# Part to part in a four-layer trunk: squares summed block by block, the boundary products by segments with the norm between them

## The chip, the cores and the metric

The kernel runs on one core of one Trainium2 chip. A core has a matrix engine (TensorE, PE in the profile), a vector engine (VectorE, DVE), a scalar engine (ScalarE, ACT), a general engine (GpSimd, POOL) and an engine that only issues transfers here (SyncE, SP). Each engine works through its own queue in order and waits on semaphores for the others. The metric is the device time of one execution in microseconds (us), lower is better.

## The reference, cut to what matters

512 tokens of 1024 features (256 of context and 256 latent ones) go through four layers, whose mixers are HGRN2, RWKV-7, MLA and HGRN2. Each layer is a mixer and a convolutional feed-forward part, each behind a norm with a shift, scale and gate of its own, which are computed from a conditioning vector:

```python
mod_l = jnp.split((silu_c @ w_mod[layer] + b_mod[layer])[:, None, :], 6, axis=-1)
h_l = modulate(rmsnorm(x_l, norm1[layer]), mod_l[0], mod_l[1])
y_c, y_l = hgrn2_mixer(h_c, h_l, ...)       # or rwkv7_mixer, or mla_mixer
x_l = x_l + mod_l[2] * y_l
x_l = x_l + mod_l[5] * conv_ffn(modulate(rmsnorm(x_l, norm2[layer]), mod_l[3], mod_l[4]), ...)
```

The context stream does the same with its own modulation; the last layer is needed for the latent tokens alone, and a last norm ends it. `conv_ffn` is a product to twice 2816 features, a convolution over three tokens, a gate and a product back to 1024. So there are eight norms, each of which needs the whole result of the part before it: the mean of squares runs over all 1024 features of a token.

## The kernel before, in words

The residual stream stays on the chip as eight tiles `xT` of 128 features x 512 tokens. Columns 0 to 255 are the context (segment 0), columns 256 to 511 the latent tokens (segment 1). Weights are loaded in single precision and split into a high part (`whi`, a cast on ScalarE, line 431) and a rest (`wlo`, a subtraction on VectorE, line 432); activations are split in the same way (`hh` and `hl`, `uh` and `ul`, `oh` and `ol`). Each product is three matmuls (`mm3`, lines 456 to 458). `dense2` (460) computes two blocks of 128 features for all 512 tokens, eight of 128 deep or eleven; a raw weight tile is `wraw`, in a ring of four.

A norm is `norm_mod` (527), which calls `rstd` (500). ScalarE squares the eight tiles (508); GpSimd adds up tiles 1 to 3, VectorE 5 and 6 (512); 12 matmuls with a column of ones per segment of 256 tokens (24 in all) give the sums (517); five small operations make the reciprocal root (`rsqrt`, 489 to 494); four matmuls spread it over the partitions (524). Then for each tile and segment VectorE scales (549), ScalarE makes `hh` (551) and VectorE `hl` (552). All this stands as a whole between the last product of one part and the first of the next; the residual is `xT[n] += gate * product` (566), on VectorE, as each block's product ends.

A scheduler with a model of the engines orders the instructions of all engines from the program and the rings of buffers; the RWKV scan is ordered by hand. What a ring of buffers allows thus sets how far loads and their users may stand apart.

The first feed-forward part (FFN 0) does two things beside its own work, in steps that `ffn` takes between its products. `presplit` (435) loads and splits RWKV's weights by way of GpSimd's queue (`praw`, `phi`, `plo`) and writes them to device memory. `mod_in_pool` (406) computes the modulation of layer 1: `mod` (383) loads 96 tiles `mraw` of 128x512 on SyncE's queue (396), eight per step, and multiplies each by the 32 columns of `sc` (397). Its ring has eight buffers. The modulation of layer 0 is computed in the same way in the first HGRN part.

## Time and profile before

| | us |
|---|---|
| median of 3 runs | 3153.69 |
| lowest, highest | 3151.88, 3156.07 |
| the profiled execution | 3154.18 |
| span of its trace | 3152.4 |
| TensorE busy | 2875.8 (91%) |
| VectorE busy | 1767.0 (56%) |
| ScalarE busy | 1391.1 (44%) |
| GpSimd busy | 552.2 (18%) |

The parts in the trace: HGRN 0 to 428, FFN 0 to 833, RWKV to about 1633, FFN 1 to 2009, MLA to 2273, FFN 2 to 2649, the last HGRN to 2935, FFN 3 to 3137, the last norm to the end. The rows below come from four views: the page (sums over the execution), a table of stretches (each engine's busy time in a stretch, with the granted TensorE clock as a share of full speed), a timeline of one engine (runs of equal instructions, and in brackets how long the engine stood idle before and for whom), and a list of the instructions of one line. Matmuls overlap in their ends, so the distance of two starts is what one costs.

### The profile page before, as it was taken

Reading aid. Unit: us, or ns where it says so; the run is one execution under the profiler, and the core shown is the slowest. Engines: PE = TensorE matmul, PEld = TensorE weight load, DVE = VectorE, ACT = ScalarE, POOL = GpSimd, SP = SyncE. Lnnn points to the kernel's source line nnn. Section 1 sums busy time; section 2 is a strip of 40 time slices with the busy share of each in tenths; the row PEclk is TensorE's granted clock in tenths of the full one; section 3 lists DMA queues with packets and bytes.
Section 4 is the critical chain, followed back from the end, with each engine's and each line's share of the span. In section 5 each row is a group of like instructions: output and inputs, shape, how many; then the busy total and the mean of one; then the engine's idle time right before and its main releaser. Section 6 shows DMA issues by size and latency. Waiting matters only on the chain. (4 is left out here: it accounts for less than half of the span.)

```text
span 3152.4 us, 52606 instructions
## 1 busy us (share of the span) xinstructions
PE 2875.8 (91%) x20861; PEld 2292.2 (73%) x20861; DVE 1767.0 (56%) x3113; ACT 1391.1 (44%) x2642; POOL 552.2 (18%) x727
## 2 busy tenths in 40 slices
PE   7999999999787787788879999899899999999898
PEld 4588877778575556666658888776578887888898
DVE  4278765445573346866564444466554344488765
ACT  3266643334442145665543223345433233577544
POOL 1023322222442133444310000000000000123000
PEclk9999989999888888988779999899999998999999
DMA  8622168886756865666553332210123332332554
GB/s 282 197 68 68 52 220 269 282 283 221 223 178 200 235 194 156 172 173 182 166 169 94 100 94 91 76 41 30 54 80 101 94 94 80 87 94 77 155 185 127
DMA packets 475336, 452.70 MB, mean 144 GB/s; under 512 B 98492, under 2 KB 415826, under 8 KB 474962
## 3 DMA queue, kind: packets, MB, share of 16 engines
q1 hardware_dynamic: 458352, 398.27, 41.3%
q0 software_dynamic: 15360, 50.34, 4.8%
q8 instruction: 164, 2.69, 0.4%
q10 hardware_dynamic: 1378, 0.73, 0.1%
q14 instruction: 82, 0.67, 0.1%
HBM read 392.64 MB, written 56.10 MB: 142 GB/s over the span
## 5 line engine op out<-in xcount | busy, mean ns | idle before, releaser
L457 PE MATMUL mm<-hl,whi 128*128 128x512 f32 (+1 forms) x2024 | 744.9, 368 | 10.9 <-DVE hl L552 10.9
L456 PE MATMUL mm<-hh,whi 128*128 128x512 f32 (+1 forms) x2024 | 744.8, 373 | 10.3 <-ACT hh L551 6.9
L458 PE MATMUL mm<-hh,wlo 128*128 128x512 f32 (+1 forms) x2024 | 742.4, 368 | 0.0
L432 DVE TENSOR_TENSOR wlo<-wraw,whi 128x1024 fp32r<-128x1024 f32 (+1 forms) x392 | 464.7, 1188 | 428.9 <-ACT whi L431 415.6
L431 ACT CAST whi<-wraw 128x1024 fp32r<-128x1024 f32 (+1 forms) x392 | 395.9, 1013 | 554.0 <-PE mm L457 489.6
L456 PEld LDWEIGHTS mm<-hh,whi 128*128 128x128 f32 x2024 | 386.2, 192 | 91.1 <-issue 10.8
L457 PEld LDWEIGHTS mm<-hl,whi 128*128 128x128 f32 x2024 | 386.0, 191 | 79.2 <-DVE hl L552 14.4
L458 PEld LDWEIGHTS mm<-hh,wlo 128*128 128x128 f32 x2024 | 385.6, 191 | 66.1 <-issue 6.1
L456 PE MATMUL mm<-uh,whi 128*128 128x512 f32 (+1 forms) x704 | 255.2, 363 | 0.0
L457 PE MATMUL mm<-ul,whi 128*128 128x512 f32 (+1 forms) x704 | 255.1, 363 | 0.0
L458 PE MATMUL mm<-uh,wlo 128*128 128x512 f32 (+1 forms) x704 | 254.2, 363 | 0.0
L512 POOL TENSOR_TENSOR t<-t,t 128x512 f32<-128x512 f32 (+1 forms) x27 | 35.2, 1305 | 868.1 <-ACT t L508 866.8
L456 PEld LDWEIGHTS mm<-uh,whi 128*128 128x128 f32 x704 | 132.8, 189 | 24.1 <-issue 2.5
L457 PEld LDWEIGHTS mm<-ul,whi 128*128 128x128 f32 x704 | 132.9, 189 | 20.3
L458 PEld LDWEIGHTS mm<-uh,wlo 128*128 128x128 f32 x704 | 132.5, 189 | 20.6
L449 DVE TENSOR_TENSOR plo<-praw,phi 128x512 fp32r<-128x512 f32 x64 | 45.3, 709 | 171.4 <-ACT phi L448 171.3
L448 ACT CAST phi<-praw 128x512 fp32r<-128x512 f32 x64 | 39.8, 622 | 216.3 <-DMA praw<-in_rw_w_rkv_dram 119.7
L2128 DVE SCALAR_TENSOR_TENSOR t<-mm,prm,t 128x510 f32<-128x510 f32 (+1 forms) x88 | 60.0, 682 | 105.4 <-ACT t L2126 105.4
L566 DVE SCALAR_TENSOR_TENSOR xT<-mm,mod,xT 128x256 f32<-128x256 f32 x176 | 74.4, 478 | 67.2 <-PE mm L458 67.2
L2126 ACT ACTIVATE t<-mm,prm 128x512 f32<-128x512 f32 (+1 forms) x88 | 63.3, 719 | 108.2 <-PE mm L458 108.2
L725 POOL TENSOR_TENSOR t<-t 128x512 f32<-128x512 f32 x32 | 46.4, 1450 | 362.6 <-DVE t L715 319.3
L1889 PE MATMUL md<-mraw,sc 128*32 128x256 f32 x768 | 71.5, 449 | 29.6 <-DMA mraw<-in_w_mod_dram 29.3
(426 smaller groups left out, 5199.7 us busy)
## 6 DMA issues: line engine op xcount, KB each, us to landing
wraw<-in_ffn_w_in_dram SPq DMA_DIRECT2D x176, 512.0 KB
mraw<-in_w_mod_dram SPq DMA_DIRECT2D x192, 256.0 KB
mraw<-in_w_mod_dram SPq DMA_DIRECT2D x96, 512.0 KB
wraw<-in_hg_w_in_dram SPq DMA_DIRECT2D x80, 512.0 KB
wraw<-in_ffn_w_out_dram SPq DMA_DIRECT2D x80, 512.0 KB
ow<-preo SPq DMA_DIRECT2D x64, 256.0 KB
praw<-in_rw_w_rkv_dram POOLq DMA_DIRECT2D x48, 256.0 KB, 4.4
vw<-prev SPq DMA_DIRECT2D x32, 256.0 KB
```

The costliest lines, as they stand in the source:

```text
L431: nc.scalar.copy(h, r)
L432: nc.vector.tensor_tensor(out=w, in0=r, in1=h.bitcast(F32), op=ALU.subtract)
L448: nc.scalar.copy(hi, raw)
L449: nc.vector.tensor_tensor(out=lo, in0=raw, in1=hi.bitcast(F32), op=ALU.subtract)
L456: nc.tensor.matmul(ps, lhsT=wh, rhs=xh, start=start, stop=False)
L457: nc.tensor.matmul(ps, lhsT=wh, rhs=xl, start=False, stop=False)
L458: nc.tensor.matmul(ps, lhsT=wl, rhs=xh, start=False, stop=stop)
L566: nc.vector.scalar_tensor_tensor(out=self.xT[n][:, sl], in0=ps[:, sl], scalar=m[:, which * 8 + n, s:s + 1], in1=self.xT[n][:, sl], op0=ALU ...
L725: nc.gpsimd.tensor_tensor(out=c3(de), in0=b3[:, :, end:end + 1].to_broadcast([P, 8, 64]), in1=b3, op=ALU.subtract)
L1889: nc.tensor.matmul(g["ps"][32 * c:32 * c + 32, halves[f]], lhsT=self.sc[:, k, :], rhs=g["raw", u][:, c], start=k == 0 and f == 0, stop=k = ...
L2126: nc.scalar.activation(c[:, sl], pa[b][:, sl], AF.Identity, bias=self.prm[:, cb + j + b:cb + j + b + 1], scale=w[1])
L2128: nc.vector.scalar_tensor_tensor(out=c3[:, :, 1:], in0=p3[:, :, :255], scalar=w[0], in1=c3[:, :, 1:], op0=ALU.mult, op1=ALU.add)
```

## The change

Four things change. First, as each block's product ends, `settle` adds it to the stream, and squares it at once; the squares of blocks 1 to 5 are added to those of block 0 (`acc`), blocks 6 and 7 keep their own tile. A norm then needs 6 sum matmuls per segment. Second, the last pair of blocks of a part goes by segments (`dense2s`, `last_pairs`; in HGRN `last_few`, all eight blocks of the last two heads), and so does the first product of the next part (`arrive`, and a piece of `hgrn`), so each of these products has 256 columns instead of 512. Third, the norm is a generator, `norm_tail`, one per segment: segment 0's stands among the products of segment 1 that end a part, segment 1's among the products of segment 0 that begin the next. Ahead of RWKV, which needs no split operands, `norm_whole` does the same work by segments. The first norm of all and the one behind RWKV stay as they were. Fourth, the tiles between two parts live in a pool of their own (`nq`), and rings elsewhere are smaller: `wraw` three instead of four in HGRN and MLA, the modulation's `mraw` in FFN 0 four instead of eight, `u` 32 instead of 34, two in HGRN by one; MLA's `p` and `q` share the ring `h`. The diff, without the pieces that only pass names on:

```diff
-HG_T2 = 13
+HG_T2 = 12
...
+    def settle(self, l, which, n, src, segs, last):
+        nc = self.nc
+        m, _ = self.mods[l]
+        sl = slice(SEGS[segs[0]][0], SEGS[segs[-1]][1])
+        x = self.xT[n]
+        for s in segs:
+            q = slice(*SEGS[s])
+            nc.vector.scalar_tensor_tensor(out=x[:, q], in0=src(s), scalar=m[:, which * 8 + n, s:s + 1], in1=x[:, q], op0=ALU.mult, op1=ALU.add)
+        if n == 0 and "acc" not in self.sq:
+            self.sq["acc"] = self.nq.tile([P, NT], F32, tag="acc", name="acc", bufs=1)
+        if n == 0:
+            nc.scalar.activation(self.sq["acc"][:, sl], x[:, sl], AF.Square)
+            return
+        if last:
+            if n not in self.sq:
+                self.sq[n] = self.nq.tile([P, NT], F32, tag="sq", name="sq", bufs=2)
+            nc.scalar.activation(self.sq[n][:, sl], x[:, sl], AF.Square)
+            return
+        if len(segs) == 1:
+            t = self.nq.tile([P, 256], F32, tag="xn", name="xn", bufs=2)
+        else:
+            t = self.nq.tile([P, NT], F32, tag="sq", name="sq", bufs=2)
+        nc.scalar.activation(t, x[:, sl], AF.Square)
+        a = self.sq["acc"]
+        nc.vector.tensor_tensor(out=a[:, sl], in0=a[:, sl], in1=t, op=ALU.add)
...
+    def norm_stat(self, segs, psum):
+        nc = self.nc
+        toks = [j for s in segs for j in (2 * s, 2 * s + 1)]
+        st = psum()
+        for i, (k, sq) in enumerate(self.sq.items()):
+            for j in toks:
+                nc.tensor.matmul(st[:, j:j + 1], lhsT=sq[:, j * P:(j + 1) * P], rhs=self.ones[:, 0:1], start=(i == 0 and j == toks[0]),
+                                 stop=(i == len(self.sq) - 1 and j == toks[-1]))
+        return self.rsqrt(st[:, toks[0]:toks[-1] + 1], [P, len(toks)], 1.0 / D, EPS)
...
+    def norm_spread(self, rr, segs, psum):
+        bc = psum()
+        j0 = 2 * segs[0]
+        for j in range(j0, 2 * segs[-1] + 2):
+            self.nc.tensor.transpose(bc[:, j * P:(j + 1) * P], rr[:, j - j0:j - j0 + 1].to_broadcast([P, P]), self.ident)
+        return bc
...
+    def norm_tail(self, l, w, h, s, psum):
+        nc = self.nc
+        m, g1 = self.mods[l]
+        rr = self.norm_stat([s], psum[0])
+        yield
+        bc = self.norm_spread(rr, [s], psum[-1])
+        sl = slice(*SEGS[s])
+        for k in range(KT):
+            hi, lo = h[k]
+            xn = self.nq.tile([P, 256], F32, tag="xn", name="xn", bufs=2)
+            sh = m[:, 24 * w + k, s:s + 1]
+            nc.vector.scalar_tensor_tensor(out=xn, in0=self.xT[k][:, sl], scalar=g1[:, 8 * w + k, s:s + 1], in1=bc[:, sl], op0=ALU.mult, op1=ALU.mult)
+            nc.scalar.activation(hi[:, sl], xn, AF.Identity, bias=sh)
+            nc.vector.scalar_tensor_tensor(out=lo[:, sl], in0=xn, scalar=sh, in1=hi[:, sl].bitcast(F32), op0=ALU.add, op1=ALU.subtract)
...
+    def leave(self, l, which, segs, nxt, blocks, psum):
+        nl, nw = nxt
+        self.table()
+        h = self.norm_tiles() if nw is not None else None
+        first = iter(())
+        for s in segs:
+            for done in blocks(s):
+                for n, src in done:
+                    self.settle(l, which, n, lambda _: src, [s], n >= KT - 2)
+                next(first, None)
+            for _ in first:
+                pass
+            if s != segs[-1]:
+                first = self.norm_tail(nl, nw, h, s, psum) if nw is not None else iter([self.rr.append(self.norm_stat([s], psum[0]))])
+        if nw is None:
+            self.rr.append(self.norm_stat([segs[-1]], psum[0]))
+        self.next = h
+        self.tail = (lambda psum: self.norm_tail(nl, nw, h, segs[-1], psum)) if nw is not None else None
...
+    def dense2s(self, wap, c0, k0, xs, segs, step, ps=None):
+        v = wap.rearrange("(k p) n -> p k n", p=P)
+        nk = len(xs)
+        g = []
+        for ks in range(0, nk, 4):
+            ke = min(ks + 4, nk)
+            g.append((ks, ke, *self.weights(v[:, k0 + ks:k0 + ke, c0:c0 + 256], ke - ks, 256)))
+        for s in segs:
+            sl = slice(*SEGS[s])
+            p = [self.psmm(), self.psmm()] if ps is None else ps
+            for ks, ke, wh, wl in g:
+                for k in range(ks, ke):
+                    for b in range(2):
+                        self.mm3(p[b][:, sl], wh[:, k - ks, b * P:(b + 1) * P], wl[:, k - ks, b * P:(b + 1) * P],
+                                 xs[k][0][:, sl], xs[k][1][:, sl], k == 0, k == nk - 1)
+                if ke < nk:
+                    yield None
+            yield p
...
+    def arrive(self, wap, c0, segs, psum):
+        tail = self.tail(psum)
+        ps = [self.psmm(), self.psmm()]
+        if len(segs) == 1:
+            for _ in tail:
+                pass
+        for _ in self.dense2s(wap, c0, 0, self.next, segs, None, ps):
+            next(tail, None)
+        for _ in tail:
+            pass
+        return ps
...
-            self.open_w(st)
+            self.open_w(st, 3)
...
                 os_.append(self.hg_read(j, o, g, sl, hp))
-            for h0, h1 in ((0, HG_A), (HG_A, 8)):
-                self.out_proj(l, a["hg_w_o"][j], h0, os_[h0:h1], sl, segs)
+            self.out_proj(l, a["hg_w_o"][j], 0, os_[:HG_A], sl, segs)
+            self.last_few(l, 2, a["hg_w_o"][j], HG_A, os_[HG_A:], segs, (l, 1), [lambda: self.psax("rd", HG_RD), lambda: self.psax("at", HG_AT)],
+                          lambda u: self.psmm() if u < 3 else self.psax("S", HG_S))
...
+    def last_pairs(self, l, which, wap, k0, xs, sl, segs, nxt, psum, step=None):
+        self.sq = {}
+        self.rr = []
+        for nb in range(0, KT - 2, 2):
+            if step:
+                step()
+            ps = self.dense2(wap, nb * P, k0, xs, sl)
+            for b in range(2):
+                self.settle(l, which, nb + b, lambda s, b=b: ps[b][:, slice(*SEGS[s])], segs, False)
+        steps = self.dense2s(wap, (KT - 2) * P, k0, xs, segs, None)
+        def blocks(s):
+            for p in steps:
+                if p is None:
+                    yield ()
+                    continue
+                yield [(KT - 2 + b, p[b][:, slice(*SEGS[s])]) for b in range(2)]
+                return
+        self.leave(l, which, segs, nxt, blocks, psum)
...
+    def last_few(self, l, which, wap, k0, xs, segs, nxt, psum, banks):
+        self.sq = {}
+        self.rr = []
+        v = wap.rearrange("(k p) n -> p k n", p=P)
+        nk = len(xs)
+        g = [self.weights(v[:, k0:k0 + nk, c0:c0 + NT], nk, NT) for c0 in (0, NT)]
+        def blocks(s):
+            sl = slice(*SEGS[s])
+            for u in range(4):
+                ps = banks(u)
+                wh, wl = g[u // 2]
+                for b in range(2):
+                    c = slice((2 * (u % 2) + b) * P, (2 * (u % 2) + b + 1) * P)
+                    for k in range(nk):
+                        self.mm3(ps[:, 256 * b:256 * b + 256], wh[:, k, c], wl[:, k, c], xs[k][0][:, sl], xs[k][1][:, sl], k == 0, k == nk - 1)
+                yield [(2 * u + b, ps[:, 256 * b:256 * b + 256]) for b in range(2)]
+        self.leave(l, which, segs, nxt, blocks, psum)
...
-        t = self.t2("rd", 4)
+        t = self.t2("rd", 3)
...
+    def norm_whole(self, l, tiles):
+        nc = self.nc
+        m, g1 = self.mods[l]
+        for s in range(2):
+            sl = slice(*SEGS[s])
+            bc = self.norm_spread(self.rr[s], [s], self.psax)
+            for k in range(KT):
+                xn = self.t2()
+                nc.vector.tensor_tensor(out=xn[:, sl], in0=self.xT[k][:, sl], in1=bc[:, sl], op=ALU.mult)
+                nc.scalar.activation(tiles[k][:, sl], xn[:, sl], AF.Identity, scale=g1[:, k, s:s + 1], bias=m[:, k, s:s + 1])
+        return tiles
...
+                    ps = self.arrive(W, 0, segs, sc)
+                    h = self.next
                 bc = self.rstd(ps, 256, 1.0 / 256, EPS, [0, 1, 2, 3], ("sc", ML_SC))
                 xs = []
                 for b in range(2):
...
-                    p = self.t2("p", ML_P)
+                    p = self.nq.tile([P, NT], F32R, tag="h", name="p", bufs=16).bitcast(F32)
...
-            nxt = iter(()) if mod is None else self.mod_in_pool(mod, st, 8)
+            nxt = iter(()) if mod is None else self.mod_in_pool(mod, st, 4 if pre else 8)
...
                     next(nxt, None)
                     steps(4)
-                    pa = self.dense2(a["ffn_w_in"][l], j * P, 0, h, sl)
+                    if j or self.tail is None:
+                        pa = self.dense2(a["ffn_w_in"][l], j * P, 0, h, sl)
+                    else:
+                        pa = self.arrive(a["ffn_w_in"][l], 0, segs, ax)
                     ss = []
                     for b in range(2):
...
-                        hi = ap.tile([P, NT], F32R, tag="u", name="uh", bufs=34)
-                        lo = ap.tile([P, NT], F32R, tag="u", name="ul", bufs=34)
+                        hi = ap.tile([P, NT], F32R, tag="u", name="uh", bufs=FF_U)
+                        lo = ap.tile([P, NT], F32R, tag="u", name="ul", bufs=FF_U)
...
                         us.append((hi, lo))
-                for nb in range(0, KT, 2):
+                def step():
                     next(nxt, None)
                     steps(3)
+                if j0:
+                    self.last_pairs(l, 5, a["ffn_w_out"][l], j0, us, sl, segs, nxt_norm, ax, step)
+                    for g in (nxt, spl):
+                        for _ in g:
+                            pass
+                    continue
+                for nb in range(0, KT, 2):
+                    step()
                     ps = self.dense2(a["ffn_w_out"][l], nb * P, j0, us, sl)
```

On TensorE in FFN 0, before, the modulation's products (`ax<-mraw,sc`) stand eight together between the products of the part:

```order
1879 L456 MATMUL mm<-hh,whi 128x512
1880 L457 MATMUL mm<-hl,whi 128x512
1881 L458 MATMUL mm<-hh,wlo 128x512
1882 L397 MATMUL ax<-mraw,sc 32x512 x8
1883 L456 MATMUL mm<-hh,whi 128x512
1884 L457 MATMUL mm<-hl,whi 128x512
1885 L458 MATMUL mm<-hh,wlo 128x512
1886 L456 MATMUL mm<-hh,whi 128x512
```

There are 11 such rows of eight, and two of four around the norm. After the change the same engine has there, a few products apart:

```order
1980 L398 MATMUL ax<-mraw,sc 32x512 x4
1981 L457 MATMUL mm<-hh,whi 128x512
1982 L458 MATMUL mm<-hl,whi 128x512
```

```order
2004 L459 MATMUL mm<-hh,wlo 128x512
2005 L398 MATMUL ax<-mraw,sc 32x512
2006 L457 MATMUL mm<-hh,whi 128x512
2007 L458 MATMUL mm<-hl,whi 128x512
2008 L459 MATMUL mm<-hh,wlo 128x512
2009 L457 MATMUL mm<-hh,whi 128x512
2010 L458 MATMUL mm<-hl,whi 128x512
2011 L398 MATMUL ax<-mraw,sc 32x512
2012 L459 MATMUL mm<-hh,wlo 128x512
2013 L457 MATMUL mm<-hh,whi 128x512
2014 L458 MATMUL mm<-hl,whi 128x512
2015 L398 MATMUL ax<-mraw,sc 32x512
```

Of the 96 products, 12 rows now have four, one three, and 45 one.

On VectorE, at the norm from FFN 1 to MLA, before (the four operations `rs` are the reciprocal root, `t` and `hl` make the operands of the next product, `wlo` is a weight split):

```order
1540 L494 SCALAR_TENSOR_TENSOR rs_18792<-rs_18793,rs_18792 128x4
1541 L549 SCALAR_TENSOR_TENSOR t_18805<-xT_81,g_8615,sc 128x256 x2
1542 L549 SCALAR_TENSOR_TENSOR t_18814<-xT_82,g_8615,sc 128x256 x2
1543 L549 SCALAR_TENSOR_TENSOR t_18823<-xT_83,g_8615,sc 128x256 x2
1544 L549 SCALAR_TENSOR_TENSOR t_18832<-xT_84,g_8615,sc 128x256 x2
1545 L552 SCALAR_TENSOR_TENSOR hl<-t_18805,mod,hh 128x256 x2
```

```order
1555 L552 SCALAR_TENSOR_TENSOR hl<-t_18859,mod,hh 128x256 x2
1556 L552 SCALAR_TENSOR_TENSOR hl<-t_18868,mod,hh 128x256 x2
1557 L432 TENSOR_TENSOR wlo<-wraw,whi 128x1024
```

After the change, from the middle of segment 0's operands to the first of segment 1 (`xn` is what `t` was):

```order
1592 L433 TENSOR_TENSOR wlo<-wraw,whi 128x1024
1593 L623 SCALAR_TENSOR_TENSOR hl<-xn,mod,hh 128x256
1594 L433 TENSOR_TENSOR wlo<-wraw,whi 128x1024
1595 L623 SCALAR_TENSOR_TENSOR hl<-xn,mod,hh 128x256
1596 L621 SCALAR_TENSOR_TENSOR xn<-xT_87,g_8831,ax 128x256
1597 L621 SCALAR_TENSOR_TENSOR xn<-xT_88,g_8831,ax 128x256
1598 L623 SCALAR_TENSOR_TENSOR hl<-xn,mod,hh 128x256 x2
1599 L490 TENSOR_SCALAR rs_19173<-sc 128x2
1600 L493 TENSOR_TENSOR rs_19175<-rs_19174 128x2
1601 L494 SCALAR_TENSOR_TENSOR rs_19175<-rs_19175,rs_19173 128x2
1602 L495 SCALAR_TENSOR_TENSOR rs_19174<-rs_19175,rs_19174 128x2
1603 L621 SCALAR_TENSOR_TENSOR xn<-xT_81,g_8831,sc 128x256
```

Weight splits that stood outside the norm stand between the operands of segment 0, and segment 1's root behind them.

On TensorE, at the end of the first HGRN part, the sums of segment 0 (`ones`) after the change, where `oh` and `ol` are the operands of the last two heads' products:

```order
1737 L457 MATMUL S<-oh,whi 128x256
1738 L458 MATMUL S<-ol,whi 128x256
1739 L459 MATMUL S<-oh,wlo 128x256
1740 L598 MATMUL rd<-ones,acc 128x1 x2
1741 L598 MATMUL rd<-ones,sq 128x1 x4
1742 L606 MATMUL at<-ident,rs_3979 128x128 x2
1743 L457 MATMUL mm<-hh,whi 128x256
```

Before, the products have 512 columns, and the whole norm's sums stood at the same place:

```order
1690 L457 MATMUL mm<-ol,whi 128x512
1691 L458 MATMUL mm<-oh,wlo 128x512
1692 L517 MATMUL ax<-ones,t_3961 128x1 x4
1693 L517 MATMUL ax<-ones,t_3972 128x1 x4
1694 L517 MATMUL ax<-ones,t_3980 128x1 x4
1695 L524 MATMUL ax<-ident,rs_3995 128x128 x4
1696 L397 MATMUL ax<-mraw,sc 32x512 x4
1697 L456 MATMUL mm<-hh,whi 128x512 x4
```

The sums now are six for one segment, and the first product of the next part follows its transposes.

## Rows read from the trace of the kernel before

**Rows 1.** Profile page: busy times, the weight split, one kind of load.
```profile
PE 2875.8 (91%) x20861; PEld 2292.2 (73%) x20861; DVE 1767.0 (56%) x3113; ACT 1391.1 (44%) x2642; POOL 552.2 (18%) x727
...
L432 DVE TENSOR_TENSOR wlo<-wraw,whi 128x1024 fp32r<-128x1024 f32 (+1 forms) x392 | 464.7, 1188 | 428.9 <-ACT whi L431 415.6
...
praw<-in_rw_w_rkv_dram POOLq DMA_DIRECT2D x48, 256.0 KB, 4.4
```
**Rows 2.** Stretches: PE, PEld, DVE, ACT, POOL busy (instructions), clock, DMA share, GB/s.
```profile
450.00:720.00 270.00, 269.21 (x1263) 206.70 (x1262) 130.12 (x175) 97.73 (x133) 57.70 (x107) 1.00 0.81 268
720.00:833.00 113.00, 113.00 (x500) 93.43 (x498) 55.20 (x77) 42.35 (x59) 29.11 (x54) 1.00 0.66 215
2955.00:3136.00 181.00, 181.00 (x1510) 181.00 (x1510) 117.65 (x166) 94.19 (x137) 2.21 (x3) 1.00 0.56 172
```
**Rows 3.** The same view, stretches around the norms.
```profile
428.00:450.00 22.00, 14.72 (x58) 9.66 (x58) 18.80 (x42) 12.96 (x27) 4.96 (x8) 0.64 0.90 309
833.00:858.00 25.00, 6.59 (x30) 5.91 (x29) 17.77 (x28) 16.04 (x32) 16.29 (x23) 0.58 0.99 266
858.00:890.00 32.00, 21.89 (x69) 15.78 (x70) 31.94 (x41) 14.27 (x24) 17.28 (x19) 0.74 0.42 127
2008.00:2034.00 26.00, 15.19 (x55) 12.13 (x54) 18.41 (x38) 13.42 (x28) 4.67 (x3) 0.61 0.18 50
2273.00:2296.00 23.00, 14.13 (x56) 10.95 (x55) 18.89 (x44) 11.11 (x23) 0.00 (x0) 0.63 0.22 69
2649.00:2670.00 21.00, 13.99 (x47) 11.09 (x46) 17.93 (x39) 11.69 (x25) 3.36 (x3) 0.59 0.23 76
2934.00:2951.00 17.00, 10.44 (x60) 9.32 (x60) 12.83 (x28) 8.42 (x19) 2.21 (x3) 0.70 0.41 124
```
**Rows 4.** Timeline of PE, FFN 1 to MLA (start, us, line, count, idle before).
```profile
2008.54 0.39 PE L458 MATMUL mm<-uh,wlo 128*128 128x512 f32 x1
2014.55 1.87 PE L517 MATMUL sc<-ones,t 128*128 128x1 f32 x8 [5.63 <-POOL t L512]
...
2023.07 1.11 PE L524 MATMUL sc<-ident,rs 128*128 128x128 f32 x4 [1.32 <-DVE rs L494]
2025.78 2.07 PE L456 MATMUL mm<-hh,whi 128*128 128x512 f32 x4 [1.59 <-ACT hh L551]
...
2029.39 0.63 PE L457 MATMUL mm<-hl,whi 128*128 128x512 f32 x1
2029.82 0.63 PE L458 MATMUL mm<-hh,wlo 128*128 128x512 f32 x1
```
**Rows 5.** Timeline of DVE, the same stretch.
```profile
2008.29 1.66 DVE L566 SCALAR_TENSOR_TENSOR xT<-mm,mod,xT 128x256 f32<-128x256 f32 x4 [11.34 <-PE mm L458]
2011.61 5.11 DVE L432 TENSOR_TENSOR wlo<-wraw,whi 128x1024 fp32r<-128x1024 f32 x3 [1.66 <-ACT whi L431]
...
2024.30 3.22 DVE L549 SCALAR_TENSOR_TENSOR t<-xT,g,sc 128x256 f32<-128x256 f32 x8 [1.29 <-PE sc L524]
```
**Rows 6.** Timeline of PE: modulation products, two, one and eight (two records each).
```profile
106.83 1.05 PE L397 MATMUL at<-mraw,sc 128*32 128x512 f32 x4
...
108.61 0.40 PE L458 MATMUL mm<-hh,wlo 128*128 128x512 f32 x1
108.94 1.04 PE L397 MATMUL at<-mraw,sc 128*32 128x512 f32 x2
109.91 0.50 PE L456 MATMUL mm<-hh,whi 128*128 128x512 f32 x1
...
491.31 0.39 PE L458 MATMUL mm<-hh,wlo 128*128 128x512 f32 x1
491.63 1.92 PE L397 MATMUL ax<-mraw,sc 128*32 128x512 f32 x16
493.48 0.50 PE L456 MATMUL mm<-hh,whi 128*128 128x512 f32 x1
```
**Rows 7.** Stretches as in rows 2: the heads of the last HGRN.
```profile
2670.00:2934.00 264.00, 249.88 (x1879) 219.21 (x1878) 189.30 (x350) 165.70 (x358) 62.31 (x81) 0.98 0.30 88
```

More of the change, by code (lines that the diff above doesn't have):

```diff
@@ new lines, in norm_tiles @@
+    def norm_tiles(self):
+        return [tuple(self.nq.tile([P, NT], F32R, tag="h", name="h" + n, bufs=16) for n in "hl") for _ in range(KT)]
+    def leave(self, l, which, segs, nxt, blocks, psum):
[16 more added lines that the diff above has]
+        self.tail = (lambda psum: self.norm_tail(nl, nw, h, segs[-1], psum)) if nw is not None else None
@@ L837, in hg_scan @@
         return o
+    def norm_whole(self, l, tiles):
+        nc = self.nc
+        m, g1 = self.mods[l]
+        for s in range(2):
+            sl = slice(*SEGS[s])
[5 more added lines that the diff above has]
+        return tiles
     def rwkv(self, l, segs):
@@ L898, in rw_project @@
         pp = st.enter_context(tc.tile_pool(name="pa", bufs=1, reuse_waits="tile"))
-        h = self.norm_mod(l, 0, [0, 1], None, None, tiles=[pp.tile([P, NT], F32, name=f"ph{i}") for i in range(KT)])
+        h = self.norm_whole(l, [pp.tile([P, NT], F32, name=f"ph{i}") for i in range(KT)])
         dx = []
@@ L2110, in ffn @@
             self.tp = st.enter_context(self.tc.tile_pool(name="ft", bufs=8, reuse_waits="tile"))
-            h = self.norm_mod(l, 1, segs, ap2(ap, 16), "h")
+            ax = [self.psax]
+            if self.tail is None:
+                h = self.norm_mod(l, 1, segs, ap2(self.nq, 16), "h")
+            else:
+                h = self.next
             def steps(n):
@@ L2154, in final @@
             op = st.enter_context(self.tc.tile_pool(name="eo", bufs=1, reuse_waits="tile"))
[L2155 to L2156 removed]
+            bc = self.norm_spread(self.rr[0], [1], self.psax)
             ot = [op.tile([P, D], F32, name=f"ot{j}") for j in range(2)]
@@ L2203, in trunk @@
         t.consts()
+        keep = ExitStack()
+        t.open_n(keep)
         for l in range(DEPTH):
             segs = [0, 1] if l < DEPTH - 1 else [1]
+            before = l + 1 < DEPTH and (l + 1) % 3 == 1
             if l % 3 == 0:
@@ L2208, in trunk @@
             elif l % 3 == 1:
+                keep.close()
                 t.rwkv(l, segs)
+                t.open_n(keep)
             else:
                 t.mla(l, segs)
-            t.ffn(l, segs, l + 1 if l + 1 < DEPTH and l + 1 not in t.mods else None, (l + 1) % 3 == 1 and l + 1 < DEPTH)
+            t.ffn(l, segs, l + 1 if l + 1 < DEPTH and l + 1 not in t.mods else None, before, (l + 1, None if before or l + 1 == DEPTH else 0))
+        keep.close()
         with ExitStack() as st:
```

54 lines of the change are left out of this document (39 added, 15 removed).

## The prediction

> **What bounds the kernel now.** I read the page's list of busy times first: TensorE is busy for 91% of the span, VectorE for 56% [rows 1]. An average says nothing about a place, so the second view is the table by stretches. Inside a sub-layer TensorE has no idle time at all: 269.21 of 270 us in the first channel mixer up to 720 us, 113.00 of 113 after it, 181.00 of 181 in the last one [rows 2]. There an instruction added to TensorE costs its whole time. The stretches around the norms are the opposite: from the last product of a sub-layer to the first products of the next, TensorE does little and its granted clock falls to between 0.58 and 0.74 [rows 3]. The timeline of one of them shows why [rows 4]: last product at 2008.54, the sum-of-squares matmuls at 2014.55 after 5.63 us idle for GpSimd's additions, the transposes at 2023.07, the first product at 2025.78, and then products 0.43 apart, where they are 0.226 apart before (113 us for 500 [rows 2]).
>
> How much each norm costs is the stretch minus the products in it. From [rows 3], with 28 (the 24 sums and 4 transposes of a norm) taken off each count: FFN 1 to MLA has 55 - 28 = 27 products, 27 x 0.226 = 6.1, so 26.0 - 6.1 = 19.9 us are lost. In the same way MLA to FFN 2 loses 23.0 - 28 x 0.226 = 16.7 and FFN 2 to the last HGRN 21.0 - 19 x 0.226 = 16.7. HGRN 0 to FFN 0 has 58 - 28 - 16 = 14 products and one set of eight modulation products (1.9 us, below): 22.0 - 3.2 - 1.9 = 16.9. FFN 0 to RWKV loses nearly all of 25.0 and then 32.0 - 69 x 0.226 = 16.4 more. Last HGRN to FFN 3, one segment: 60 - 12 - 2 = 46 products of 0.12 (181 us for 1510 [rows 2]), so 17.0 - 5.5 = 11.5.
>
> **The norms, gain.** In the order of the change, at FFN 1 to MLA, segment 0's sums and transposes stand among the products of segment 1, the transposes four products before the last one; its VectorE work then runs while TensorE ends the old product and starts the new one. What is late next is VectorE. Between the transposes of segment 0 and segment 1's first operand its queue holds 16 operations of 128x256, two residuals and three weight splits, as the VectorE rows of the change show in part. Durations: 8 of the 128x256 kind take 3.22 us and 4 residuals 1.66 [rows 5], so 0.40 and 0.41 each; a weight split takes 1.19 [rows 1]. 16 x 0.40 + 2 x 0.41 + 3 x 1.19 = 10.8. To it come the chain of reciprocal root, 1.3 (TensorE's idle time before the transposes [rows 4]), the sums and transposes of one segment, about 0.6 (estimate, a half of the 1.11 of four transposes and little more), and VectorE's and ScalarE's first operand, 0.40 each: 2.7. Less the 0.5 by which the transposes stand ahead, segment 1's first product comes 13.0 us after the last old one. In between TensorE has the 48 products of segment 0, 48 x 0.12 = 5.8. Lost: 7.2, and I add 2.0 for products at the lower clock (about ten at 0.43 for 0.226 [rows 4]): 9.2. Before, the three weight splits lay in the wait for GpSimd [rows 5]; now they stand in the chain that TensorE waits for. Gains: FFN 1 to MLA 19.9 - 9.2 = 10.7; MLA to FFN 2 and FFN 2 to HGRN, with like queues, 7.5 each.
>
> HGRN 0 to FFN 0 gets less: there segment 0's sums stand behind the very last product, so its chain (2.0) and its 16 operations are not covered by segment 1's products: 2.0 + 6.4 + 3.6 + 1.2 (two splits of half the size) + 2.7 = 15.9, less 5.8, plus 2.0 = 12.1: gain 4.8. FFN 0 to RWKV: VectorE is the bound from 858 to 890 (31.94 of 32 [rows 3]); from 833 to 890 it is busy 49.7 of 57, so 7.3 can be gained there, and about 2 more by the additions that move ahead: 9. Last HGRN to FFN 3 has no second segment to cover its norm: 0. The last norm saves its square additions, about 1. Sum: 10.7 + 15 + 4.8 + 9 + 0 + 1 = 40.5. For a bound from below: the 2 us of clock may be 4 in four places and the queues of VectorE may wait for ScalarE's casts, so 28; from above, below under the rivals, 63.
>
> **The modulation products, loss.** The change halves the ring of their weight tiles in the first channel mixer. 96 such products of 32 columns are there. Before, 88 of them stand outside the norm in 11 sets of eight side by side (16 records a set [rows 6], two for each). In the order of the change the second four of each eight wait for a buffer, and are spread: 58 groups instead of 13, namely 12 of four, one of three, and 45 alone, one of four being in the slack of the norm. The price of each stands in the trace. Eight together: from the product before at 491.31 to the product after at 493.48 are 2.17 us, less the 0.23 of a pair without them: 1.94. One alone, in layer 0 between the same kind of products: 108.61 to 109.91 is 1.30, less 0.23: 1.07; two side by side take no longer, 1.05 for 1.04 [rows 6]. From two on each adds some 0.15 (1.94 for eight), so a group of four is near 1.35, and one of three near 1.2. Before: 11 x 1.94 = 21.3. After: 45 x 1.07 + 11 x 1.35 + 1.2 = 64.2. Difference 42.9, in a stretch where nothing is idle [rows 2]. The groups near the ends of the part may have a wait to stand in: 40. Bounds: 30 if a part stands in waits that are there anyway, 45 where groups lie close together.
>
> **Their loads.** Twelve sets of four loads now wait for TensorE to free the ring, and the weight loads behind them on SyncE's queue wait too. A load of the same 256 KB takes 4.4 us on GpSimd's queue [rows 1]. The DMA engines are 0.81 busy there [rows 2]. If each set is waited for in full, 12 x 4.4 = 53; if none, 0. The first single stands 25 rows, some 5.7 us, behind its four, so I am near the lower end: 4.
>
> **Split products.** The order has 516 products of 512 columns fewer and 1032 of 256 more. A pair of 0.12 is 0.24 for 0.226: 516 x 0.014 = 7, of which some stand in the stretches counted above: 5. Bounds 0 and 13. The Trainium skill, "TensorEngine Tiling (Array Packing)", Instruction Overhead, gives each matmul an overhead of about 60 cycles; at the upper clock of 2.4 GHz 516 more would by that be 13 us (an estimate from that page). The rows at 0.12 and 0.226 show half as much, and the sum goes by them.
>
> **Smaller rings in HGRN and MLA** (weights 4 to 3, two others by one). Over the heads of the last HGRN TensorE is idle for 264.0 - 249.9 = 14.1 us [rows 7], so its tiles are mostly there early. A buffer less can delay, and another order can help: -3 to 8, taken as 2.
>
> **Sum.** Against the profiled execution of 3154.18 us (span 3152.4 and 1.8 around it; the median of the runs is 3153.69, 0.5 less): 3154.2 + 40 + 4 + 5 + 2 - 40 = 3165. I forecast 3165 us, slower by 0.35%. About 0.2%, 6.3 us, is what a measurement of this kernel can tell from no change. Its own range, by the bounds of the terms taken together, is 3152 to 3182.
>
> **Rivals.**
> Faster (other side): the clock. If the products of segment 0 are enough that the granted clock stays at full, and the weight splits slip into VectorE's gaps, each of the three wide boundaries loses about 5 us rather than 9.2, HGRN 0 to FFN 0 also 5, and FFN 0 to RWKV gains 12: 14.9 + 11.7 + 11.7 + 11.9 + 12 + 1 = 63. Then 3154.2 + 51 - 63 = 3142. It decides for faster once the gains pass 57. For it: the last HGRN to FFN 3, with the shortest idle times, shows 0.70, FFN 0 to RWKV 0.58 [rows 3]. Against: it fell there too, after a wait of about 6 us, and 13.0 us with 5.8 of products leave a longer one. The Trainium skill, "TensorE: Matmul & The Clock Gate", What's actually happening, says that the array is throttled by default and that activity releases it: by that rule filling the gap keeps the clock, which is this rival. The trace agrees that the clock falls in every norm, and no row shows it with the gap half filled.
>
> Loads waited for: TensorE's queue is in order, and a modulation product whose load is late holds all behind it. At three quarters of the 53: 3165 - 4 + 40 = 3201, say 3200. For it: DMA is 0.81 busy. Against: the scheduler has put the singles some microseconds behind the fours.
>
> No change that counts: the singles cost less than the row shows, since the products around them, in a denser stretch, are ready to go (0.8 a group: 46 - 21 = 25), and the gains are as summed: 3154.2 + 25 + 11 - 38 = 3152. Against: the row of 1.30 was taken among just such products.
>
> **Chances.** Forecast 0.52, faster by the clock 0.20, no change 0.15, loads 0.13. The forecast's own spread (3152 to 3182) puts a fifth of it, 0.09, within 6.3 us, and 0.03 of the no-change case lies below: faster 0.23, same 0.21, slower 0.56. The range is 3143 to 3195: it reaches to the clock's 3142 but not past it, and short of the full wait for loads.
>
> **What would show it.** In the profile after: isolated modulation products between products 1.30 us apart, and the first channel mixer longer by some 40; the stretch from the last product of FFN 1 to full rate in MLA shorter by about 10, with TensorE waiting for VectorE's segment 1 and a granted clock below 1; no idle time for GpSimd's additions. Wrong would be: singles that cost 0.3 to 0.5, a clock of 1 across the norms, or TensorE waiting for the modulation loads in microseconds.

## The result, and the profile after

The changed kernel takes 3187.5 us (median of 4 runs, 3180.8 to 3192.4), the kernel before 3152.8: 1.0108 times as long, 95% interval 1.0085 to 1.0131. The profiled execution took 3192.37, with a span of 3190.7, so it is the slowest of the four.

Where the time went shows in the distance from the last product of a part to the last product of the next (starts of these products, from the timelines of TensorE; each part holds the norm at its start):

```
us              HGRN 0  FFN 0   RWKV  FFN 1    MLA  FFN 2  HGRN 3  FFN 3
before           428.0  404.8  797.3  378.4  264.6  376.1   285.9  201.9
after            421.6  452.4  796.7  382.2  269.8  371.9   281.1  200.7
difference        -6.4  +47.6   -0.6   +3.8   +5.2   -4.2    -4.8   -1.2
```

FFN 0 alone lost more than the whole kernel. The stretches of the changed kernel that answer to [rows 2, 3], shifted with the parts (span, then busy time and instructions of PE, PEld, DVE, ACT, POOL, then clock, DMA share, GB/s):

```profile
421.00:443.00 22.00, 11.92 (x74) 10.71 (x73) 15.56 (x34) 9.95 (x20) 3.34 (x7) 0.74 0.81 273
450.00:720.00 270.00, 270.00 (x1121) 180.02 (x1120) 119.43 (x160) 92.64 (x126) 57.83 (x108) 1.00 0.78 257
720.00:874.00 154.00, 154.00 (x722) 121.76 (x721) 74.83 (x112) 57.14 (x82) 32.72 (x64) 1.00 0.62 203
874.00:899.00 25.00, 6.68 (x26) 3.84 (x24) 22.63 (x40) 14.18 (x28) 13.55 (x17) 0.59 0.98 251
899.00:931.00 32.00, 26.88 (x102) 20.67 (x103) 31.94 (x33) 15.22 (x24) 18.41 (x11) 0.89 0.35 116
2053.00:2079.00 26.00, 21.70 (x139) 19.60 (x138) 19.42 (x43) 13.64 (x28) 0.00 (x0) 0.93 0.29 84
2323.00:2346.00 23.00, 18.65 (x110) 16.86 (x109) 18.19 (x41) 12.34 (x24) 0.00 (x0) 0.85 0.30 94
2695.00:2716.00 21.00, 15.23 (x102) 14.52 (x103) 16.46 (x37) 11.11 (x23) 2.48 (x8) 0.84 0.24 76
2976.00:2993.00 17.00, 10.21 (x70) 9.69 (x70) 14.44 (x31) 9.77 (x18) 0.00 (x0) 0.80 0.54 173
```

Two things are to be seen. In the 270 us from 450, TensorE is busy throughout as before, but weight loads fell from 1262 to 1120 [rows 2]: fewer products in the same time, with no engine to wait for. And around the wide norms TensorE is busier: 21.70 of 26 us where it was 15.19 [rows 3], with a granted clock of 0.93 for 0.61.

In between stand the lone modulation products, on TensorE in FFN 0:

```profile
551.64 0.39 PE L459 MATMUL mm<-hh,wlo 128*128 128x512 f32 x1
551.96 1.05 PE L398 MATMUL ax<-mraw,sc 128*32 128x512 f32 x2
552.94 0.50 PE L457 MATMUL mm<-hh,whi 128*128 128x512 f32 x1
553.27 0.39 PE L458 MATMUL mm<-hl,whi 128*128 128x512 f32 x1
...
554.29 1.04 PE L398 MATMUL ax<-mraw,sc 128*32 128x512 f32 x2
555.27 0.50 PE L459 MATMUL mm<-hh,wlo 128*128 128x512 f32 x1
```

From 551.64 to 552.94 is 1.30 us, as in layer 0 before [rows 6]. Groups of four cost the same 1.31, not the 1.58 (1.35 and 0.23) of my estimate; why is in the last section. No product here waits for its load. At FFN 1 to MLA, which answers to [rows 4]:

```profile
2052.33 0.38 PE L606 MATMUL ax<-ident,rs 128*128 128x128 f32 x2
...
2052.90 0.28 PE L459 MATMUL mm<-uh,wlo 128*128 128x256 f32 x1
2056.26 0.58 PE L457 MATMUL mm<-hh,whi 128*128 128x256 f32 x1 [3.08 <-DVE xn L621]
...
2062.73 0.50 PE L598 MATMUL sc<-ones,acc 128*128 128x1 f32 x4
2063.09 1.03 PE L598 MATMUL sc<-ones,sq 128*128 128x1 f32 x8
...
2065.53 0.40 PE L606 MATMUL sc<-ident,rs 128*128 128x128 f32 x2
2067.05 0.97 PE L457 MATMUL mm<-hh,whi 128*128 128x256 f32 x4 [1.11 <-ACT hh L622]
```

Segment 0's transposes stand before the last old product (2052.90), its first new product comes 3.4 us after it, segment 1's 14.1 us after it; the prediction had 13.0. GpSimd's wait is gone. On VectorE the operands of segment 0 and the weight splits stand close behind each other up to segment 1's reciprocal root:

```profile
2060.49 1.22 DVE L433 TENSOR_TENSOR wlo<-wraw,whi 128x1024 fp32r<-128x1024 f32 x1
2061.62 0.48 DVE L623 SCALAR_TENSOR_TENSOR hl<-xn,mod,hh 128x256 fp32r<-128x256 f32 x1
2062.02 0.87 DVE L621 SCALAR_TENSOR_TENSOR xn<-xT,g,ax 128x256 f32<-128x256 f32 x2
2063.07 0.89 DVE L623 SCALAR_TENSOR_TENSOR hl<-xn,mod,hh 128x256 fp32r<-128x256 f32 x2 [0.18 <-ACT hh L622]
2064.16 0.16 DVE L490 TENSOR_SCALAR rs<-sc 128x2 f32<-128x2 f32 x1 [0.21 <-PE sc L598]
```

HGRN 0 to FFN 0 is the norm that got no better. TensorE's waits there, then ScalarE's and VectorE's rows that explain them:

```profile
424.47 0.47 PE L606 MATMUL at<-ident,rs 128*128 128x128 f32 x2 [1.35 <-DVE rs L495]
430.10 0.58 PE L457 MATMUL mm<-hh,whi 128*128 128x256 f32 x1 [5.16 <-ACT hh L622]
...
439.56 0.60 PE L598 MATMUL ax<-ones,acc 128*128 128x1 f32 x4 [2.90 <-DVE acc L589]
```

```profile
428.07 0.62 ACT L449 CAST phi<-praw 128x512 fp32r<-128x512 f32 x1 [3.32 <-DMA praw<-in_rw_w_rkv_dram]
428.60 1.04 ACT L432 CAST whi<-wraw 128x1024 fp32r<-128x1024 f32 x1
429.55 0.50 ACT L622 ACTIVATE hh<-xn,mod 128x256 fp32r<-128x256 f32 x1
```

```profile
445.24 0.69 DVE L450 TENSOR_TENSOR plo<-praw,phi 128x512 fp32r<-128x512 f32 x1 [3.98 <-ACT phi L449]
445.85 0.15 DVE L493 TENSOR_TENSOR rs<-rs 128x2 f32<-128x2 f32 x1
```

VectorE has scaled the first two tiles at 426.8, but ahead of `hh` in ScalarE's queue stands a cast of RWKV's weight preparation that waits 3.32 us for its load. Segment 1's reciprocal root waits on VectorE behind the next one, 3.98 us.

### The profile page after: what moved, and what is told of

It is laid out like the page before. It is cut to its first block, busy times and chain, and to the rows that moved or that the text cites. A ratio compares the mean times of both kernels' runs of the same rounds, so it can differ in the third digit from the quotient of the medians.

```text
span 3190.7 us, 53662 instructions
## 1 busy us (share of the span) xinstructions
PE 2926.0 (92%) x21377; PEld 2317.2 (73%) x21377; DVE 1783.4 (56%) x3163; ACT 1396.4 (44%) x2668; POOL 526.4 (16%) x706
## 3 DMA queue, kind: packets, MB, share of 16 engines
q1 hardware_dynamic: 458288, 398.27, 40.2%
## 4 chain that ended last, share of the span: by engine, by line
PE 75%; DVE 8%; DMA 7%; ACT 4%; issue 4%; POOL 1%; SPq 1%; ACTq 0%; DVEq 0%; POOLq 0%
PE mm L457 18%; PE mm L458 18%; PE mm L459 18%; PE ax L398 2%; DMA mraw<-in_w_mod_dram 2%; DMA praw<-in_rw_w_o_dram 1%; PE sc L2247 1%; PE at L398 1%; DMA vw<-prev 1%; PE md L2091 1%; PE ax L1543 1%; PE at L1025 1%; PE o L2279 1%; DMA praw<-in_rw_w_rkv_dram 1%; DVE t L1125 1%
## 5 line engine op out<-in xcount | busy, mean ns | idle before, releaser
L458 PE MATMUL mm<-hl,whi 128*128 128x512 f32 (+1 forms) x2088 | 756.0, 363 | 4.0 <-DVE hl L553 3.3
L458 PEld LDWEIGHTS mm<-hl,whi 128*128 128x128 f32 x2088 | 399.8, 192 | 76.1 <-issue 14.5
L459 PEld LDWEIGHTS mm<-hh,wlo 128*128 128x128 f32 x2088 | 399.0, 191 | 71.9 <-issue 12.6
L457 PE MATMUL mm<-uh,whi 128*128 128x512 f32 (+1 forms) x764 | 266.7, 350 | 0.0
L458 PE MATMUL mm<-ul,whi 128*128 128x512 f32 (+1 forms) x764 | 266.4, 349 | 0.0
L459 PE MATMUL mm<-uh,wlo 128*128 128x512 f32 (+1 forms) x764 | 265.3, 349 | 0.0
L457 PEld LDWEIGHTS mm<-uh,whi 128*128 128x128 f32 x764 | 144.5, 189 | 27.3 <-issue 8.4
L458 PEld LDWEIGHTS mm<-ul,whi 128*128 128x128 f32 x764 | 144.6, 189 | 23.7 <-issue 5.9
L459 PEld LDWEIGHTS mm<-uh,wlo 128*128 128x128 f32 x764 | 144.2, 189 | 19.5 <-issue 1.7
L2348 DVE TENSOR_TENSOR t<-t,mm 128x512 f32<-128x512 f32 (+1 forms) x88 | 54.0, 620 | 62.0 <-PE mm L459 61.8
```

Of the source, the lines that this page charges most:

```text
L457: nc.tensor.matmul(ps, lhsT=wh, rhs=xh, start=start, stop=False)
L458: nc.tensor.matmul(ps, lhsT=wh, rhs=xl, start=False, stop=False)
L459: nc.tensor.matmul(ps, lhsT=wl, rhs=xh, start=False, stop=stop)
L2348: nc.vector.tensor_tensor(out=ss[b][:, sl], in0=ss[b][:, sl], in1=pv[b][:, sl], op=ALU.mult)
```

## The experiments

Times are medians; a ratio is against the kernel before on the same chip, with its 95% interval.

**One. The ring of four alone, in the kernel before.**

```diff
-            nxt = iter(()) if mod is None else self.mod_in_pool(mod, st, 8)
+            nxt = iter(()) if mod is None else self.mod_in_pool(mod, st, 4 if pre else 8)
```

> The kernel before with one edit: the ring of modulation tiles in FFN 0 has four buffers instead of eight. Theory (spread products): the second four of each eight then stand alone between full products, 57 groups at 1.07 us and more instead of 11 of 1.94, so FFN 0 goes from 404.8 us to about 447 and the whole from 3153 to about 3195. Rival (the ring is harmless, FFN 0 got longer by the norm between the parts and the products by segments): 3153, FFN 0 at 405.

Measured: 3195.8 to 3155.8, ratio 1.0140 (1.0104 to 1.0176). FFN 0 took 447.9 for 404.8, 43.1 more. Its part behind the norm:

```profile
458.02:875.89 417.87, 417.87 (x1732) 293.05 (x1730) 183.30 (x244) 141.58 (x192) 90.27 (x168) 1.00 0.74 241
```

TensorE has no idle time in it, so the loads are not late: the spread products themselves take the time. At the prices of the trace (1.08 a group, 1.94 a set of eight) 57 groups for 11 sets are 40.2 of the 43.1; the rest was not traced. One number of the change does the damage, without any of the rest.

**Two. Eight buffers in the changed kernel.**

```diff
-            nxt = iter(()) if mod is None else self.mod_in_pool(mod, st, 4 if pre else 8)
+            nxt = iter(()) if mod is None else self.mod_in_pool(mod, st, 8)
-                        hi = ap.tile([P, NT], F32R, tag="u", name="uh", bufs=FF_U)
+                        hi = ap.tile([P, NT], F32R, tag="u", name="uh", bufs=FF_U - 2 * pre)
```

(`ul` likewise.) 

> The changed kernel with eight buffers again, room for them made by a ring u of 30 instead of 32 in FFN 0. Spread products: the sets of eight are back, FFN 0 goes from 452.4 to about 411 and the whole from 3187 to about 3146, below the kernel before. Rival (segments and norm, or the ring u, lengthen FFN 0): it stays above 3180.

Measured: 3158.5 to 3155.8, ratio 1.0011 (0.9991 to 1.0030). FFN 0 takes 413.3, 39.1 less. The sets are back:

```profile
586.24 1.92 PE L398 MATMUL ax<-mraw,sc 128*32 128x512 f32 x16
```

The mechanism held. The whole missed the 3146 expected: on this chip the kernel before took 3155.8, 3 more, and the runs of this kernel spread from 3145.7 to 3162.7, which is wider than the miss (RWKV's time varies most from profile to profile: last section). So without the ring of four the rest of the change is worth nothing that can be told from no change: FFN 0 is still 8.6 longer than before, and the parts that got shorter make up for it.

**Three. Four buffers, steps of four.**

```diff
-                if k % 2 == 0:
+                if k % every == 0:
                     yield
...
+                    if pre:
+                        next(nxt, None)
                     pv = self.dense2(a["ffn_w_in"][l], DFF + j * P, 0, h, sl)
```

(`every` is 1 where the ring has four buffers, else 2.) 

> The changed kernel with its four buffers, but the modulation stepped four products at a time, twice per pair of blocks, so that a step never needs a fifth buffer: 22 rows of four instead of 12 and 45 alone. If the number of switches to the 32-column products is what costs (about 1.08 a row), FFN 0 falls by some 57 x 1.08 - 26 x 1.08 = 33 us and the whole to about 3154. If the four buffers cost by late loads, it stays at 3187, with TensorE waiting for the modulation's loads.

Measured: 3176.4, ratio 1.0059 (1.0034 to 1.0083); FFN 0 431.6, 20.8 less than 452.4 where 33 were expected. TensorE's waits in FFN 0 (what waited, for whom, us in total, times, longest):

```profile
PE ax L404 <- ACT modev L401: 9.8, 2, 8.4
```

So the fewer groups gave most of what was worked out (26 stand there, 22 of them of four), and about 10 us came back as a wait for ScalarE's copy of the sums, which now stands behind, among others, a preparation cast that waits 2.17 us for its load. Grouping helps without more room; how much depends on what the new places push. Each group here is one switch to the narrow products and one round of them through the engine, so this experiment doesn't tell which of the two is paid for (last section).

**Four. MLA's shared ring, in the kernel before.**

```diff
-                q_s = self.t2("q", 2)
+                q_s = hp.tile([P, NT], F32, tag="pq", name="q", bufs=16)
-                    p = self.t2("p", ML_P)
+                    p = hp.tile([P, NT], F32, tag="pq", name="p", bufs=16)
```

> The kernel before with one edit in MLA: p and q share one ring of 16 instead of rings of 10 and 2, as in the change. MLA takes 264.6 us before and 269.7 after, though the norm ahead of it got 11 shorter, so 15 were lost inside. If the shared ring lost them (it sets another order of the heads), MLA here takes 275 to 280 and the whole 3163 to 3168. If the three raw weight buffers or the segments did, it stays at 265 and 3153.

Measured: 3152.0, ratio 0.9995 (0.9978 to 1.0013); MLA 266.3 for 264.6. By the total the ring was acquitted. But its heads, from the first score to the last weighted sum, took 184.4 us for 174.8, as they did after the change (185.4); they began 8 us earlier (55.8 after the last product of FFN 1 for 63.7), which hid it. The reading of the total alone would have misled; experiment eight settles it.

**Five. RWKV's weight preparation held back** (in the kernel of experiment two).

```diff
-                    steps(4)
+                    steps(5 if j else 0)
...
-                    nc.scalar.copy(hi, raw)
+                    cast = nc.scalar.copy(hi, raw)
+                    if n == "k" and k < 2:
+                        self.tc.keep_in_program_order(cast)
```

> The changed kernel with eight buffers (as before this) and RWKV's weight preparation held back: its first casts on ScalarE keep their place in the program, which is behind the norm from HGRN 0 to FFN 0, and start with the second pair of blocks. Theory (the norm between HGRN 0 and FFN 0 gained nothing since its operands and its reciprocal root stand in the in-order queues behind casts that wait for a load: 5.2 us before the first product, 7.3 before the second transposes): that stretch loses about 9 us instead of 17 to 18, FFN 0 goes from 413.3 to about 405, the whole from 3158 to about 3150. Rival (VectorE's own work bounds that norm, as for the other three): FFN 0 stays at 411 or more.

Measured: 3193.5, ratio 1.0114 (1.0091 to 1.0137). The norm did get better, TensorE being busy for 22.98 us of the first 30 (first row) instead of 18.42 in the changed kernel (second) and 19.57 in experiment two, but FFN 0 stayed at 415.6, so the rival's figure came true, and RWKV went from 790.3 to 835.4:

```profile
420.60:450.60 30.00, 22.98 (x123) 18.51 (x121) 20.24 (x48) 12.51 (x27) 0.00 (x0) 0.77 0.67 222
```

```profile
421.69:451.69 30.00, 18.42 (x108) 15.43 (x107) 19.44 (x45) 13.00 (x27) 5.03 (x10) 0.77 0.73 247
```

The last casts of the preparation on ScalarE, and what TensorE waited for in that stretch:

```profile
898.26 0.62 ACT L449 CAST phi<-praw 128x512 fp32r<-128x512 f32 x1 [5.43 <-DMA praw<-in_rw_w_o_dram]
904.43 0.62 ACT L449 CAST phi<-praw 128x512 fp32r<-128x512 f32 x1 [5.55 <-DMA praw<-in_rw_w_o_dram]
...
938.66 0.62 ACT L449 CAST phi<-praw 128x512 fp32r<-128x512 f32 x1 [5.07 <-DMA praw<-in_rw_w_o_dram]
```

```profile
PE ax L1217 <- ACT kp L1215: 45.6, 1, 45.6
```

The preparation is a chain of 64 loads through one buffer, about 460 us from its first cast to its last in experiment two, somewhat longer than FFN 0 itself. Started 75 us later it ends inside RWKV, eight casts in ScalarE's queue each wait 5 us for a load, and TensorE's work waits behind them. The casts in the norm are a real cost to the norm, but moving them costs more in RWKV. What FFN 0 would gain stays open: it took 413.3 in experiment two and 417.9, with the same edits in FFN 0, in experiment eight, so 415.6 says little on a difference of a few us.

**Six. All smaller rings of HGRN and MLA, in the kernel before.**

```diff
-HG_T2 = 13
+HG_T2 = 12
...
+            self.wraw = 3
-        t = self.t2("rd", 4)
+        t = self.t2("rd", 3)
```

(Three raw weight buffers in both, MLA's ring as in experiment four.) 

> The kernel before with the change's smaller rings alone: three raw weight buffers in HGRN and MLA, the two other HGRN rings by one less, p and q of MLA in one ring of 16. The changed kernel's first HGRN part was 6.3 us shorter and its MLA 5.2 longer though its norm ahead got 11 shorter. If the rings (the order they set) do both, HGRN 0 here takes 421 to 423 and MLA 275 or more. If the parts by segments do, HGRN 0 stays at 428 and MLA at 265 to 267.

Measured in a single run: 3171.2. HGRN 0 took 442.0, not 421 to 423: in the freed room RWKV's preparation is issued from 5 us on instead of 391 (GpSimd, which issues it, is busy for 131.7 us of the last 277 of HGRN 0, 80.6 of 263 before), so this says nothing on HGRN 0's 6.4 us. The last HGRN took 292.0, 6 longer than before, so the smaller rings alone lengthen it there. MLA took 270.2, as the change's does, but with the old, longer norm ahead of it.

**Seven. Two loads in flight for the preparation, and four raw weight buffers in MLA** (in the kernel of experiment two).

```diff
-                    raw = pool.tile([P, NT], F32, tag="praw", name="praw", bufs=1)
+                    raw = pool.tile([P, NT], F32, tag="praw", name="praw", bufs=2)
...
-            self.open_w(st, 3)
+            self.open_w(st)
```

(The second in MLA; room from ring `u`, 28, and two spare tiles of MLA.) 

> The changed kernel with eight modulation buffers, and two more edits in other stretches. In FFN 0 the loads of RWKV's weight preparation get two buffers instead of one (room from ring u, 28). Theory (the norm from HGRN 0 to FFN 0 waits because casts ahead in ScalarE's queue wait for a load that can only start when the one buffer is free): the waits of 5.2 and 7.3 us go, FFN 0 falls from 413.3 to 404 to 408. Rival (the casts and splits themselves fill the queues): 412 or more. In MLA four raw weight buffers again (room from two spare tiles): if the third buffer cost the 4 us by which the kernel with both smaller rings was longer than the one with the shared ring alone (270.2 to 266.3), MLA falls from 270 to 266; if the shared ring and the earlier start do it, it stays at 270. The whole, by both: 3158 - 7 - 4 = 3147, under 3155 of before.

Measured: 3163.9, ratio 1.0042 (1.0026 to 1.0058). Both parts failed. FFN 0 rose to 428.1, and the norm still waits, now on other transfers of the same preparation (VectorE, then ScalarE):

```profile
428.24 0.69 DVE L450 TENSOR_TENSOR plo<-praw,phi 128x512 fp32r<-128x512 f32 x1 [4.27 <-DMA prek<-plo]
```

```profile
429.28 0.62 ACT L449 CAST phi<-praw 128x512 fp32r<-128x512 f32 x1 [4.86 <-DMA praw<-in_rw_w_rkv_dram]
```

MLA stayed at 270.1. Here too the total hides two shifts: the heads took 180.8 us for the 185.6 of experiment two, but began 4.0 later. So this doesn't show that the third raw buffer is harmless; only that giving it back, with two spare tiles less, gains nothing in all.

**Eight. MLA's p and q on twelve fixed tiles of the shared ring** (in the kernel of experiment two).

```diff
+            pq = [self.nq.tile([P, NT], F32R, tag="h", name="pq", bufs=16).bitcast(F32) for _ in range(12)]
-                q_s = self.nq.tile([P, NT], F32R, tag="h", name="q", bufs=16).bitcast(F32)
+                q_s = pq[10 + hd % 2]
-                    p = self.nq.tile([P, NT], F32R, tag="h", name="p", bufs=16).bitcast(F32)
+                    p = pq[(4 * hd + q) % 10]
```

> The changed kernel with eight modulation buffers (ring u 30 in FFN 0), and in MLA p and q on 12 fixed tiles of the shared ring, ten and two in turn, as before the change. Theory (the ring of 16 lets the scores run further ahead of their transposes, by 2.6 heads in the order instead of 1.9, and the heads then take 185 us from the first score to the last weighted sum instead of 175): the lead is 1.8 here, the heads take about 175, MLA falls from 270.8 to about 261, the whole from 3158 to about 3148, under 3155 of before by 0.2%. Rival (the heads are as long whatever the ring, since something else ends MLA at 265 to 270 after the last product of FFN 1): MLA stays at 268 or more.

Measured: 3145.1 to 3156.6, ratio 0.9977 (0.9962 to 0.9993), so this version is 0.23% faster than the kernel before, about as little as can be told here. MLA takes 261.5 (expected 261), its heads 175.1 (expected 175). TensorE's waits in MLA behind the norm, in the changed kernel and in this one:

```profile
PE pt L2266 <- ACT pt L2268: 8.8, 13, 0.7
```

```profile
PE pt L2266 <- ACT pt L2268: 3.9, 7, 0.7
```

Before the change this wait was 3.9 us, 7 times, too. So the ring's reach sets the order: with more tiles the scheduler puts more scores first (at a transpose the scores are on average 2.1 heads ahead in the kernel before, 3.0 in the changed one and 2.0 here), and the transposes, which go through one buffer that ScalarE and VectorE empty, stand closely behind each other. The wait in the two rows is 4.9 of the 9.3 us that MLA gets shorter from experiment two to this one.

## Why the prediction was right, and where it was not

The direction and the range held (3187.5 in 3143 to 3195), on the mechanism that was forecast. The size, 3165, was 22 short.

*Modulation products, +40.* Shown: experiments one and two give 43.1 and 39.1 in FFN 0. That the 40 was met so well is in part luck: I priced a group of four at 1.35 where it costs 1.08, which is 3 too much for eleven of them, and took 3 off for waits that they might stand in; there were none. The reading behind it, that each product after the first adds some 0.15, was wrong: four run side by side, and a group pays 0.87 for each round of up to four and about 0.20 for the way in and out (last section). The Trainium skill, "TensorEngine Tiling (Array Packing)", Key Properties, says that a change of the tiling mode drains TensorE. The trace agrees as far as that 0.20 of the 1.07 us goes; the larger part of the loss is rounds with one product where four fit. The rival of cheaper singles is out: none in FFN 0 took less than 1.29 us from the product before to the product after.

*Their loads, +4.* Measured at nothing: TensorE is busy for all of the 270 us. The rival of late loads is out.

*Norms, -40.5.* By TensorE's time in each stretch less its products, within about 1 us:

```
                   FFN1-MLA  MLA-FFN2  FFN2-HGRN  HGRN0-FFN0  FFN0-RWKV  HGRN-FFN3  last
forecast gain          10.7       7.5        7.5         4.8          9          0     1
measured gain          11.3       6.5        5.8        -1.7   11, then 0      1.2   1.6
```

The 24 sums of the working are records, two for each matmul: before as after, a norm takes six sum matmuls per segment, so no gain lies there. The three wide norms came within 2 us, and the reason was right: VectorE's queue sets when segment 1 starts. Their clock fell less than I took, 0.84 to 0.93, which is half of the rival of the clock; it was not full, and the gain was that of the forecast. Two steps failed. For HGRN 0 to FFN 0 I counted two preparation splits as VectorE's work and not the loads that they wait for, though they stand in the same in-order queues; the rows of after show 3.32 and 3.98 us of that. FFN 0 to RWKV did gain: the first product comes 14.1 us after the last old one (873.98), not 25.2 (832.81). The first row is before, the second after:

```profile
857.99 0.79 PE L456 MATMUL mm<-xh,whi 128*128 128x512 f32 x1 [10.43 <-ACT xh L415]
```

```profile
888.07 0.80 PE L457 MATMUL mm<-xh,whi 128*128 128x512 f32 x1 [8.34 <-ACT xh L416]
```

But RWKV as a whole took 796.7 for 797.3. The lead is 10 us where its scan begins, about 3 in the middle and 0.3 at its end. That the gain must reach the end of RWKV was an unspoken step of the sum, and these two profiles don't show it. Nor do they refute it: over all profiles, RWKV without a held-back preparation took 789.1 to 797.3 with the old entry and 787.2 to 798.5 with the new one. Experiment four, whose text is that of the kernel before up to MLA, took 8.2 less in RWKV than the kernel before, and experiment eight, with the new entry, still has a lead of 10 over the kernel before at the end. The scan's own spread is as large as the gain, so what became of it stays open. These two places are 15 of the 22 us (6.5 and 8.4).

*Split products, +5.* FFN 1 from its first product to its last grew from 365.4 to 367.6, by 2.2; its 60 split products are 0.8 by the price. The term as a whole was not measured by itself.

*Smaller rings, +2.* The mis-sized step. I priced a buffer less as a tile that comes late. What a ring does here is to change the order that the scheduler finds: the one that mattered became larger, not smaller. The shared ring of 16 for MLA's p and q cost the 9.3 us between experiments two and eight. MLA thus became 5.2 longer though its norm ahead gave 11.3 back. Without that ring it is 3.1 shorter than before, so some 8 us more are lost inside it: 5.7 between the norm and the first score, 2.2 behind the last weighted sum. About 1.3 of them (96 x 0.014) are split products; the rest stays open. The last HGRN is 4.8 shorter, but its norm alone gave 5.8, so nothing is gained inside it. HGRN 0 has no changed norm ahead of it and is 6.4 shorter, which I had not in the sum. These waits of TensorE in its last 263 us, before, are gone after the change:

```profile
PE tr L749 <- DVE t L745: 6.8, 5, 1.6
```

Which edit took the five away was not found; experiment six can't tell it.

## What to carry to other kernels

Price an instruction by what stands beside it: nearly the same products cost 21 us in eleven sets of eight and 61 in 57 groups, since a round of the matrix engine takes as long with one narrow product in it as with four. When room is taken from a ring to pay for something, count first what the ring kept together, or kept apart, and read the new order at its user. A norm that is laid over other work is only as early as the slowest transfer that anything ahead of it in an in-order queue waits for.
